# Inverting the odd layer's triangles by blocks of 16 instead of 32

## Chip, cores and metric

One core of one Trainium2 chip runs the whole program. The metric is device time in microseconds for one execution, lower is better. TensorE multiplies matrices, VectorE and ScalarE work on SBUF and on the products in PSUM, GpSimd (POOL) helps, and SyncE (SP) issues the transfers.

## What is computed

A decoder trunk of two layers on 1024 tokens of width 1024, in float32: an even layer (dilated window attention beside a gated linear recurrence), then an odd layer (gated DeltaNet), then a norm. The change lies in the odd layer. Per head and per chunk of 64 tokens the reference solves a unit lower triangular system:

```
lower = jnp.where(strict, jnp.einsum('bhnid,bhnjd->bhnij', kb, kc) * decay, 0.0)
a_mat = lower + jnp.eye(C_CHUNK, dtype=jnp.float32)
rhs = jnp.concatenate([vc * bc, kb * jnp.exp(gcum)[..., None]], axis=-1)
sol = lax.linalg.triangular_solve(a_mat, rhs, left_side=True, lower=True, unit_diagonal=True)
...
v_new = u_n - jnp.einsum('bhcd,bhdv->bhcv', w_n, state)
o = jnp.einsum('bhcd,bhdv->bhcv', qd_n, state) + jnp.einsum('bhij,bhjv->bhiv', a_n, v_new)
new_state = state * gl_n[..., None, None] + jnp.einsum('bhcd,bhcv->bhdv', kt_n, v_new)
```

The chunk length is free, as the result is the same recurrence; the kernel takes chunks of 128 tokens.

## The kernel before

The odd layer has 16 value heads that share 8 key heads. The kernel works on them in 8 pairs, `hh` = 0 to 7. For each pair it projects and convolves k, v and q (`proj`, `conv`), inverts the pair's 16 triangles of 128x128 (8 chunks by 2 heads; `invert`), and then walks the 8 chunks in turn (`recur`), where `ks`, `r`, `vp`, `vt`, `kv` and `S` form a chain over the chunks: TensorE, VectorE, TensorE, VectorE, and so on. `way_out` normalizes and gates a finished pair (`oz`, `ot`) and stores it for the last projection.

`invert` builds the triangles `L` from `kk`, the products of the keys, in two batches. It copies the 32x32 diagonal blocks to `Lg` and turns them with VectorE (`Lp`), so that each of the 128 partitions holds one block's column, 16 blocks of one partition group in the free dimension. A forward substitution of 31 steps on VectorE (`tm`, then `Tp`, two operations per step) inverts all 64 blocks at once. `Tn` and `Un` are the inverse and its transpose. From there TensorE doubles the block size with small products: `qp` and `up` from 32 to 64, `q2` and `u2` (in the trace `q` and `u`) from 64 to 128. All these products share one PSUM bank, tag "c". `T0`, the start of `Tp`, is loaded from a table of constants through SP.

TensorE's order is no loop nest. `invert` and `recur` are generators; `blend` and `mix` let projection work (`fill`) run between their steps. A step yields a need, in us of other work that should cover its latency, and what it does itself:

```
            for need, did in side:
                yield did
                debt += need * scale
```

A scheduler then fixes one order per engine when the program is built, from its own estimate of when operands are ready. In each engine's queue that order is kept on the chip. Hence every operation of the chain waits for whatever the order has put ahead of it on its engine.

While pair `hh` goes through `recur`, `invert(hh + 1)` and `proj(hh + 1)` run between its steps. Pair 0 is inverted ahead of all recurrences.

Of the kernel before, what the change touches and what calls it, by code (L numbers as in the profile page):

```python
# [9 lines left out]
F32 = mybir.dt.float32  # L10
F32R = mybir.dt.float32r
BF16 = mybir.dt.bfloat16
I32 = mybir.dt.int32
AF = mybir.ActivationFunctionType
ALU = mybir.AluOpType
# [3 lines left out]
P = 128  # L19
# [16 lines left out]
C_LV = C_MA + 128  # L36
C_ID32 = C_LV + 5 * 16
C_T0 = C_ID32 + 32
C_ALL = C_T0 + 512


def const_table():
    c = np.zeros((P, C_ALL), np.float32)
    p = np.arange(P)
    c[:, C_ID:C_ID + 128] = np.eye(P)

    a, q = p // 32, p % 32 * 4 + p // 32

    def count(dist):
        cnt = np.zeros(dist.shape, np.int64)  # L50
        for window, dil in ((128, 1), (512, 4), (2048, 16)):
# [12 lines left out]
    for lv in range(5):  # L64
        s = 1 << lv
        blk = j // s
        i = np.arange(32)
        odd = i[(i // s) % 2 == 1]
        c[:, C_LV + 16 * lv:C_LV + 16 * lv + 16] = (blk[:, None] % 2 == 0) & (blk[:, None] + 1 == odd[None, :] // s)
    c[:, C_ID32:C_ID32 + 32] = j[:, None] == np.arange(32)[None, :]  # L70

    i, j = np.arange(32)[:, None], np.arange(16)[None, :]
    for par in range(2):
        c[(p // 16) % 2 == par, C_T0:C_T0 + 512] = (i == 2 * j + par).reshape(-1)
    return c


# [1 line left out]
def trunk_kernel(ctx: ExitStack, tc: tile.TileContext, x, ew, ewo, ow, owab, owo, nw, fnw, lbl, hnw,  # L79
# [660 lines left out]
    def odd_layer(es):  # L740
        sp = es.enter_context(tc.tile_pool(name="od", bufs=1))
        gt = {n: sp.tile([P, NT, 16], F32, name=f"g_{n}") for n in ("beta", "gc", "ngc", "eg", "nbeg", "etl", "egl")}
        MA = sp.tile([P, 128], F32, name="MA")
        nc.sync.dma_start(MA, cst[:, C_MA:C_MA + 128])
        cws = sp.tile([P, 32, 4], F32, name="cws")
        nc.sync.dma_start(cws, cw)
        ow_ = sp.tile([P, 1], F32, name="onws")
# [219 lines left out]
        def invert(hh):  # L967
            kT = KT[hh]

            L = sp.tile([P, 16, 128], F32, name=f"L{hh}", tag="L", bufs=2)  # L970
            Lg = sp.tile([P, 16, 32], F32, name=f"Lg{hh}", tag="Lg")

            def decay_l(c):
                gcB = decays(hh, c, "l")

                for e in range(2):
                    act.activation(gcB[:, e, :], gcB[:, e, :], AF.Relu, bias=gt["ngc"][:, c, 2 * hh + e:2 * hh + e + 1])
                act.activation(gcB, gcB, AF.Exp, scale=-1.0)
                return gcB

            ahead_l = [decay_l(0)]
            for h in range(2):
                kk = bank("c", [P, 4, 128], f"kk{hh}_{h}")
                for c in range(4 * h, 4 * h + 4):
                    k_ = kT[:, c * 128:(c + 1) * 128]
                    pe.matmul(kk[:, c - 4 * h, :], k_, k_, start=True, stop=True)
                for c in range(4 * h, 4 * h + 4):
                    gcB = ahead_l.pop()
                    if c < NT - 1:
                        ahead_l.append(decay_l(c + 1))  # L990
                    for e in range(2):
                        dve.scalar_tensor_tensor(L[:, 2 * c + e, :], kk[:, c - 4 * h, :], SC[hh][:, 0, c, e:e + 1],
                                                 gcB[:, e, :], op0=ALU.mult, op1=ALU.mult)
                yield (15 if h else 7.0), 0.9


            for b in range(4):
                r = slice(32 * b, 32 * b + 32)
                act.copy(Lg[r], L[r, :, r])
            Lp = sp.tile([P, 32, 32], F32, name=f"Lp{hh}", tag="LpQ")  # L1000
            dve.transpose(Lp, Lg.rearrange("p u j -> p j u")[:, :, None, :].to_broadcast([P, 32, 2, 16]))
            Tp = sp.tile([P, 32, 16], F32, name=f"Tp{hh}", tag="Tp")
            nc.sync.dma_start(Tp, cst[:, C_T0:C_T0 + 512].rearrange("p (i j) -> p i j", i=32))
            for k in range(31):
                n = k // 2 + 1
                tm = sp.tile([P, 31, 16], F32, name=f"tm{hh}_{k}", tag="tm")
                dve.tensor_tensor(tm[:, :31 - k, :n], Lp[:, k, k + 1:, None].to_broadcast([P, 31 - k, n]),
                                  Tp[:, k:k + 1, :n].to_broadcast([P, 31 - k, n]), op=ALU.mult)
                dve.tensor_tensor(Tp[:, k + 1:, :n], Tp[:, k + 1:, :n], tm[:, :31 - k, :n], op=ALU.subtract)
            Tn = sp.tile([P, 16, 32], F32, name=f"Tn{hh}", tag="tm")  # L1010
            dve.transpose(Tn.rearrange("p u (j h) -> p j h u", h=2), Tp.rearrange("p i j -> p j i"))
            Un = sp.tile([P, 16, 32], F32, name=f"Un{hh}", tag="Lg")
            dve.transpose(Un, Tn)

            U = L
            T64 = sp.tile([64, 16, 64], F32, name=f"T64_{hh}", tag="T64")
            pool.memset(T64[0:32, :, 32:64], 0.0)
            for b in range(2, 4):
                r = slice(32 * b, 32 * b + 32)
                dve.tensor_copy(U[r, :, r], Un[r])  # L1020
            for b in range(2):
                r = slice(32 * b, 32 * b + 32)
                pool.tensor_copy(T64[r, :, r], Tn[r])

            a0, b0 = [slice(0, 32), slice(64, 96)], [slice(32, 64), slice(96, 128)]
            Q_ = sp.tile([P, 16, 64], F32, name=f"Q{hh}", tag="LpQ")
            qp = bank("c", [P, 16, 32], f"qp{hh}")
            for u in range(16):
                for r in range(2):
                    pe.matmul(qp[a0[r], u, :], L[b0[r], u, a0[r]], Un[b0[r], u, :], start=True, stop=True)  # L1030
            act.copy(Q_[a0[0], :, 0:32], qp[a0[0]])
            dve.tensor_copy(Q_[a0[1], :, 0:32], qp[a0[1]])
            yield 1.5, 1.3
            up = bank("c", [P, 16, 32], f"up{hh}")
            for u in range(16):
                for r in range(2):
                    pe.matmul(up[a0[r], u, :], Tn[a0[r], u, :], Q_[a0[r], u, 0:32], start=True, stop=True)
                pe.matmul(up[b0[0], u, :], Q_[a0[0], u, 0:32], Tn[a0[0], u, :], start=True, stop=True)
            act.mul(U[a0[1], :, b0[1]], up[a0[1]], -1.0)
            dve.tensor_scalar(T64[b0[0], :, 0:32], up[b0[0]], -1.0, None, op0=ALU.mult)  # L1040
            act.mul(U[a0[0], :, b0[0]], up[a0[0]], -1.0)
            for r in (1, 0):
                pool.memset(U[b0[r], :, a0[r]], 0.0)
            for b in range(2):
                r = slice(32 * b, 32 * b + 32)
                pool.tensor_copy(U[r, :, r], Un[r])

            yield 2.0, 1.8
            for h in range(2):

                q2 = bank("c", [P, 4, 64], f"q2{hh}_{h}")
                for u in range(8 * h, 8 * h + 8):
                    pe.matmul(q2[u % 2 * 64:u % 2 * 64 + 64, u // 2 % 4, :], L[64:128, u, 0:64], U[64:128, u, 64:128],
                              start=True, stop=True)
                for e in range(2):
                    (act.copy if h ^ e else dve.tensor_copy)(Q_[0:64, 8 * h + e:8 * h + 8:2, :], q2[64 * e:64 * e + 64])
                yield 1.2, 1.7
            for h in range(2):
                u2 = bank("c", [P, 4, 64], f"u2{hh}_{h}")
                for u in range(8 * h, 8 * h + 8):  # L1060
                    pe.matmul(u2[u % 2 * 64:u % 2 * 64 + 64, u // 2 % 4, :], T64[:, u, :], Q_[0:64, u, :], start=True, stop=True)
                for e in range(2):
                    d = U[0:64, 8 * h + e:8 * h + 8:2, 64:128]
                    if h ^ e:
                        act.mul(d, u2[64 * e:64 * e + 64], -1.0)
                    else:
# [203 lines left out]
```

## Time and profile before

| | |
|---|---|
| median of 3 runs | 2288.92 us (2286.33 to 2290.3) |
| profiled execution | 2290.27 us, its span 2288.5 us |
| TensorE busy, granted clock | 2171.9 us (95%), 0.993 |
| VectorE busy | 1427.0 us (62%) |
| substitution on VectorE (L1007, L1009) | 74.3 and 70.2 us in 2 x 248 operations |
| odd layer's inversions and recurrences | from about 1240 to 2126 us |

In the profile PE is TensorE, DVE VectorE, ACT ScalarE. A matmul of float32 operands shows as two records. A timeline row gives start, duration, engine, line, operation, tiles and shape, and in brackets the idle time before it and what ended it; a row of groups gives busy time, mean duration in ns of one, and idle time before; a row of windows gives a stretch, its length, and busy time of each engine with the number of records, the granted TensorE clock, the share of busy DMA and GB/s.

### The profile page before, as it was taken

What the parts mean: (1) busy time and instruction counts of PE and PEld (TensorE: products, weight loads), DVE (VectorE), ACT (ScalarE), POOL (GpSimd) and SP (SyncE); (2) the same over time, 40 slices, a digit from 0 to 9 for tenths busy, and PEclk for the clock granted to TensorE, in tenths of its full rate; (3) what the DMA queues carried; (4) which work ended last, traced back from release to release, by engine and by line L of the source; (5) the groups of instructions that cost most, each with busy time, mean ns of one, the idle gap of its engine ahead of it and who ended that gap; (6) DMA issues with size and microseconds to landing.
All of it is one profiled execution on the core that took longest, in us unless ns stands there. A gap on an engine that the chain in (4) does not pass through costs nothing. (4 is left out here: it accounts for less than half of the span.)

```text
span 2288.5 us, 54642 instructions
## 1 busy us (share of the span) xinstructions
PE 2171.9 (95%) x22597; PEld 1809.0 (79%) x22597; DVE 1427.0 (62%) x3364; ACT 963.4 (42%) x2623; POOL 226.5 (10%) x236
## 2 busy tenths in 40 slices
PE   7999999999999999988999988989899989899998
PEld 6888888898888888866887776767777767678787
DVE  6444444444444444456777887878788877855777
ACT  5333333333333332322236663755555555544223
POOL 0000000000000000000000012131212121210000
PEclk9999999999999999999999998999999999999999
DMA  4111111113222323352323221121212121214232
GB/s 145 38 48 48 44 47 48 43 39 95 78 82 84 90 83 92 97 160 88 102 97 104 59 56 62 53 79 46 76 43 76 52 74 59 65 60 148 91 113 109
DMA packets 101864, 175.83 MB, mean 77 GB/s; under 512 B 16752, under 2 KB 34032, under 8 KB 101616
## 3 DMA queue, kind: packets, MB, share of 16 engines
q1 hardware_dynamic: 101616, 172.35, 24.2%
q8 instruction: 177, 2.90, 0.5%
q14 instruction: 71, 0.58, 0.1%
HBM read 127.07 MB, written 25.23 MB: 67 GB/s over the span
## 5 line engine op out<-in xcount | busy, mean ns | idle before, releaser
L113 DVE TENSOR_TENSOR w_lo<-raww,w_hi 128x512 fp32r<-128x512 f32 x292 | 211.9, 727 | 151.1 <-ACT w_hi L112 147.1
L112 ACT CAST w_hi<-raww 128x512 fp32r<-128x512 f32 x292 | 181.1, 620 | 270.1 <-PE op L145 68.0
L143 PE MATMUL av<-w_hi,hn_hi 128*128 128x256 f32 x512 | 149.0, 291 | 0.0
L143 PE MATMUL bi<-w_hi,hn_hi 128*128 128x256 f32 x512 | 147.0, 287 | 0.0
L144 PE MATMUL bi<-w_lo,hn_hi 128*128 128x256 f32 x512 | 145.3, 284 | 0.0
L144 PE MATMUL av<-w_lo,hn_hi 128*128 128x256 f32 x512 | 144.8, 283 | 0.0
L145 PE MATMUL bi<-w_hi,hn_lo 128*128 128x256 f32 x512 | 144.8, 283 | 0.0
L145 PE MATMUL av<-w_hi,hn_lo 128*128 128x256 f32 x512 | 144.7, 283 | 0.0
L575 ACT ACTIVATE P<-P,nm 128x256 f32<-128x256 f32 (+7 forms) x128 | 71.4, 559 | 130.2 <-DVE nm L573 130.0
L143 PE MATMUL op<-w_hi,yplo 128*128 128x512 f32 x288 | 113.5, 394 | 1.6 <-DVE hr L273 0.9
L145 PE MATMUL op<-w_hi,yplo 128*128 128x512 f32 x288 | 112.2, 390 | 0.0
L144 PE MATMUL op<-w_lo,yplo 128*128 128x512 f32 x288 | 112.1, 389 | 0.0
L143 PE MATMUL pv<-hn_hi,w_hi 128*128 128x512 f32 x256 | 107.0, 418 | 2.6 <-ACT uv L822 2.6
L143 PE MATMUL oz<-hn_hi,w_hi 128*128 128x512 f32 x256 | 109.4, 427 | 0.0
L273 DVE TENSOR_TENSOR hr<-hr,op 128x512 f32<-128x512 f32 x128 | 86.1, 684 | 34.5 <-PE op L145 34.0
L145 PE MATMUL pv<-hn_hi,w_lo 128*128 128x512 f32 x256 | 104.3, 407 | 0.0
L144 PE MATMUL pv<-hn_lo,w_hi 128*128 128x512 f32 x256 | 102.6, 401 | 0.0
L144 PE MATMUL oz<-hn_lo,w_hi 128*128 128x512 f32 x256 | 102.3, 400 | 0.0
L145 PE MATMUL oz<-hn_hi,w_lo 128*128 128x512 f32 x256 | 102.0, 398 | 0.0
L581 DVE STREAM_TRANSPOSE PB<-P 128x256 f32<-128x256 f32 (+3 forms) x64 | 54.6, 854 | 74.9 <-ACT P L575 74.8
L143 PEld LDWEIGHTS av<-w_hi,hn_hi 128*128 128x128 f32 x512 | 97.9, 191 | 3.5 <-issue 1.9
L144 PEld LDWEIGHTS bi<-w_lo,hn_hi 128*128 128x128 f32 x512 | 98.1, 192 | 0.0
(354 smaller groups left out, 6044.9 us busy)
## 6 DMA issues: line engine op xcount, KB each, us to landing
raww<-in_ew_dram SPq DMA_DIRECT2D x128, 256.0 KB, 3.1
raww<-in_ow_dram SPq DMA_DIRECT2D x100, 256.0 KB, 3.0
V<-v SPq DMA_DIRECT2D x256, 64.0 KB, 2.0
rawy<-ymix SPq DMA_DIRECT2D x64, 256.0 KB, 2.7
raww<-in_ewo_dram SPq DMA_DIRECT2D x32, 256.0 KB, 3.0
gcl<-gcd SPq DMA_DIRECT2D x64, 128.0 KB, 3.0
gca<-gcd SPq DMA_DIRECT2D x64, 128.0 KB, 3.0
ymix<-oy SPq DMA_DIRECT2D x32, 256.0 KB, 2.0
```

What stands on the lines that cost most here:

```text
L112: act.copy(hi, raw)
L113: dve.tensor_tensor(lo, raw, hi.bitcast(F32), op=ALU.subtract)
L143: pe.matmul(ps, lh, rh, start=start, stop=False)
L144: pe.matmul(ps, lh, rl, start=False, stop=False)
L145: pe.matmul(ps, ll, rh, start=False, stop=stop)
L273: dve.tensor_tensor(dst[:, n], src[:, n], ps, op=ALU.add)
L575: act.activation(Pm[:, e, w0:], Pm[:, e, w0:], AF.Exp, bias=nmx[:, e:e + 1], scale=0.125, accum_out=den[:, i, e:e + 1])
L581: dve.transpose(PB[:, :, i * WG + w0:(i + 1) * WG], Pm[:, :, w0:])
```

## The change

The substitution stops at blocks of 16. The two 16x16 diagonal blocks of each 32x32 block are turned so that each partition holds a column of its own half: the transpose `Lp` is half as large, and a predicated copy with a mask `MH` (one column per half) moves the second half's rows into place. 15 steps instead of 31 follow, on at most 64 elements per partition instead of 136. ScalarE spreads the result over both halves with two masked copies, and `Tn` and `Un` are turned as before. Then comes the new doubling from 16 to 32: 64 products of 32x32 by 32x16 on the four diagonal places of the array (`sp0`), a masked copy on ScalarE (`Q0`, tile `Qs`), 64 more products (`sp1`), a subtraction into `Un`, and a second transpose that gives `Tn`. `Un` moves from `Lg`'s buffer to `Tp`'s. The need after the second batch of `kk` falls from 15 to 10, and the two new steps yield a need of 1.5 each. The load of `T0` halves; `MH` is a new small load at the layer's start.

```
-                yield (15 if h else 7.0), 0.9
+                yield (10 if h else 7.0), 0.9
...
-            Lp = sp.tile([P, 32, 32], F32, name=f"Lp{hh}", tag="LpQ")
-            dve.transpose(Lp, Lg.rearrange("p u j -> p j u")[:, :, None, :].to_broadcast([P, 32, 2, 16]))
+            Lp = sp.tile([P, 16, 32], F32, name=f"Lp{hh}", tag="LpQ")
+            dve.transpose(Lp, Lg.rearrange("p u (s j) -> p j s u", s=2))
+            dve.copy_predicated(Lp[:, :, 0:16], MH[:, 1:2, None].bitcast(I32).to_broadcast([P, 16, 16]), Lp[:, :, 16:32])
...
-            for k in range(31):
-                n = k // 2 + 1
-                tm = sp.tile([P, 31, 16], F32, name=f"tm{hh}_{k}", tag="tm")
-                dve.tensor_tensor(tm[:, :31 - k, :n], Lp[:, k, k + 1:, None].to_broadcast([P, 31 - k, n]),
-                                  Tp[:, k:k + 1, :n].to_broadcast([P, 31 - k, n]), op=ALU.mult)
-                dve.tensor_tensor(Tp[:, k + 1:, :n], Tp[:, k + 1:, :n], tm[:, :31 - k, :n], op=ALU.subtract)
+            for k in range(15):
+                n = k + 1
+                tm = sp.tile([P, 15, 16], F32, name=f"tm{hh}_{k}", tag="tm")
+                dve.tensor_tensor(tm[:, :15 - k, :n], Lp[:, k, k + 1:16, None].to_broadcast([P, 15 - k, n]),
+                                  Tp[:, k:k + 1, :n].to_broadcast([P, 15 - k, n]), op=ALU.mult)
+                dve.tensor_tensor(Tp[:, k + 1:16, :n], Tp[:, k + 1:16, :n], tm[:, :15 - k, :n], op=ALU.subtract)
+
+            act.mul(Tp[:, 16:32], Tp[:, 0:16], MH[:, 1:2])
+            act.mul(Tp[:, 0:16], Tp[:, 0:16], MH[:, 0:1])
             Tn = sp.tile([P, 16, 32], F32, name=f"Tn{hh}", tag="tm")
-            dve.transpose(Tn.rearrange("p u (j h) -> p j h u", h=2), Tp.rearrange("p i j -> p j i"))
-            Un = sp.tile([P, 16, 32], F32, name=f"Un{hh}", tag="Lg")
+            dve.transpose(Tn.rearrange("p u (s j) -> p j s u", s=2), Tp.rearrange("p i j -> p j i"))
+            Un = sp.tile([P, 16, 32], F32, name=f"Un{hh}", tag="Tp")
             dve.transpose(Un, Tn)
+
+            blk = [slice(32 * b, 32 * b + 32) for b in range(4)]
+            Q0 = sp.tile([P, 16, 16], F32, name=f"Qs{hh}", tag="LpQ")
+            sp0 = bank("c", [P, 16, 16], f"s0{hh}")
+            for u in range(16):
+                for r in blk:
+                    pe.matmul(sp0[r, u, :], Lg[r, u, :], Un[r, u, 16:32], start=True, stop=True)
+            act.mul(Q0, sp0, MH[:, 0:1])
+            yield 1.5, 1.4
+            sp1 = bank("c", [P, 16, 16], f"s1{hh}")
+            for u in range(16):
+                for r in blk:
+                    pe.matmul(sp1[r, u, :], Tn[r, u, :], Q0[r, u, :], start=True, stop=True)
+            dve.tensor_tensor(Un[:, :, 16:32], Un[:, :, 16:32], sp1, op=ALU.subtract)
+            dve.transpose(Tn, Un)
+            yield 1.5, 1.4
```

The scheduler makes a new order from this. On TensorE, around the first product that needs the inverted blocks of pair 5, this stood before (`pv` and `pk` are projections):

```order
L143 MATMUL pv_0_0_21964<-hn_hi_15183,w_hi_21213 128x512
L144 MATMUL pv_0_0_21964<-hn_lo_15185,w_hi_21213 128x512
L1030 MATMUL qp_21575<-Un_21566,L_21144 32x32 x32
L145 MATMUL pv_0_0_21964<-hn_hi_15183,w_lo_21214 128x512
...
L145 MATMUL pv_0_0_21964<-hn_hi_15183,w_lo_21214 128x512
L1105 MATMUL ks_5_21977<-S_4_21942,kT_19458 128x256
L1037 MATMUL up_21623<-Q_21574,Tn_21564 32x32 x2
```

and this stands there now, `s` being `sp0` (L1027) and `sp1` (L1033):

```order
L145 MATMUL pk_0_22353<-hn_lo_15185,w_hi_21648 128x512
L1027 MATMUL s_21908<-Un_21905,Lg_21592 32x16 x64
L1163 MATMUL op_3_22310<-vn_3_22292,A_3_22224 128x128 x2
L1114 MATMUL qk_4_22318<-q_21546,kT_19823 128x128
L1033 MATMUL s_22014<-Qs_21907,Tn_21903 32x16 x64
L1128 MATMUL ks_4_22371<-S_3_22307,kT_19823 128x256
L1134 MATMUL qs_4_22376<-S_3_22307,q_21546 128x256
L1053 MATMUL qp_22105<-Un_21905,L_21591 32x32 x32
L146 MATMUL pk_0_22353<-hn_hi_15183,w_lo_21649 128x512
```

The first product on the blocks has come a chunk earlier in the recurrence (3 instead of 4), one or two recurrence products stand behind each new pass, and `pk` is still being projected where `pv` was.

On VectorE, the end of the substitution of pair 5 stood so before:

```order
L1007 TENSOR_TENSOR tm_30_21561<-Lp_21467,Tp_21469 128x16
L1123 TENSOR_TENSOR vt_4_21917<-vp_4_21914,g_etl 128x256
L1009 TENSOR_TENSOR Tp_21469<-Tp_21469,tm_30_21561 128x16
L1011 STREAM_TRANSPOSE Tn_21564<-Tp_21469 128x32x16
L831 SCALAR_TENSOR_TENSOR kT_21894<-uk_21754,kT_21894 128x512
L1013 STREAM_TRANSPOSE Un_21566<-Tn_21564 128x512
...
L1020 COPY L_21144<-Un_21566 32x16x32 x2
L827 SCALAR_TENSOR_TENSOR kT_21894<-uk_21754,cws,kT_21894 128x512
...
L1032 COPY Q_21574<-qp_21575 32x16x32
```

and so now, with the `g` that ScalarE's masking has to let pass:

```order
L1011 TENSOR_TENSOR tm_14_21898<-Lp_21851,Tp_21854 128x15
L1013 TENSOR_TENSOR Tp_21854<-Tp_21854,tm_14_21898 128x15
L918 SCALAR_TENSOR_TENSOR g_1_1_22264<-g_1_1_22264,oz_1_1_22091 128x512
L1018 STREAM_TRANSPOSE Tn_21903<-Tp_21854 128x16x2x16
L1146 TENSOR_TENSOR vt_3_22290<-vp_3_22287,g_etl 128x256
L1020 STREAM_TRANSPOSE Un_21905<-Tn_21903 128x512
...
L1034 TENSOR_TENSOR Un_21905<-Un_21905,s_22014 128x16x16
L1131 SCALAR_TENSOR_TENSOR r_4_22373<-ks_4_22371,sc_19969,bv_21430 128x128
L1035 STREAM_TRANSPOSE Tn_21903<-Un_21905 128x512
L1043 COPY L_21591<-Un_21905 32x16x32 x2
...
L1055 COPY Q_22104<-qp_22105 32x16x32
```

The convolutions of `kT` that stood between `Un` and the copy of `Q` have moved behind it; the subtraction and a transpose have come in.

More of the change, by code (lines that the diff above doesn't have):

```diff
@@ L38 @@
 C_T0 = C_ID32 + 32
-C_ALL = C_T0 + 512
+C_MH = C_T0 + 256
+C_ALL = C_MH + 2
 def const_table():
@@ L70, in const_table @@
     c[:, C_ID32:C_ID32 + 32] = j[:, None] == np.arange(32)[None, :]
-    i, j = np.arange(32)[:, None], np.arange(16)[None, :]
-    for par in range(2):
-        c[(p // 16) % 2 == par, C_T0:C_T0 + 512] = (i == 2 * j + par).reshape(-1)
+    c[:, C_T0:C_T0 + 256] = np.eye(16).reshape(-1)
+    for half in range(2):
+        c[(p // 16) % 2 == half, C_MH + half] = 1.0
     return c
@@ L744, in odd_layer @@
         nc.sync.dma_start(MA, cst[:, C_MA:C_MA + 128])
+        MH = sp.tile([P, 2], F32, name="MH")
+        nc.sync.dma_start(MH, cst[:, C_MH:C_MH + 2])
         cws = sp.tile([P, 32, 4], F32, name="cws")
@@ L999, in invert @@
                 act.copy(Lg[r], L[r, :, r])
-            Lp = sp.tile([P, 32, 32], F32, name=f"Lp{hh}", tag="LpQ")
-            dve.transpose(Lp, Lg.rearrange("p u j -> p j u")[:, :, None, :].to_broadcast([P, 32, 2, 16]))
+            Lp = sp.tile([P, 16, 32], F32, name=f"Lp{hh}", tag="LpQ")
+            dve.transpose(Lp, Lg.rearrange("p u (s j) -> p j s u", s=2))
+            dve.copy_predicated(Lp[:, :, 0:16], MH[:, 1:2, None].bitcast(I32).to_broadcast([P, 16, 16]), Lp[:, :, 16:32])
             Tp = sp.tile([P, 32, 16], F32, name=f"Tp{hh}", tag="Tp")
-            nc.sync.dma_start(Tp, cst[:, C_T0:C_T0 + 512].rearrange("p (i j) -> p i j", i=32))
@@ L1004, in invert @@
-            for k in range(31):
-                n = k // 2 + 1
-                tm = sp.tile([P, 31, 16], F32, name=f"tm{hh}_{k}", tag="tm")
-                dve.tensor_tensor(tm[:, :31 - k, :n], Lp[:, k, k + 1:, None].to_broadcast([P, 31 - k, n]),
-                                  Tp[:, k:k + 1, :n].to_broadcast([P, 31 - k, n]), op=ALU.mult)
-                dve.tensor_tensor(Tp[:, k + 1:, :n], Tp[:, k + 1:, :n], tm[:, :31 - k, :n], op=ALU.subtract)
+            nc.sync.dma_start(Tp[:, 0:16], cst[:, C_T0:C_T0 + 256].rearrange("p (i j) -> p i j", i=16))
```

## The prediction

> **What bounds the kernel now.** I read the page first (busy times), then the windows view for one head pair cut into stages, then the windows of all eight inversions, then the timeline where a stage stood out.
>
> ```profile
> span 2288.5 us, 54642 instructions
> ...
> PE 2171.9 (95%) x22597; PEld 1809.0 (79%) x22597; DVE 1427.0 (62%) x3364; ACT 963.4 (42%) x2623; POOL 226.5 (10%) x236
> ```
>
> TensorE is 95% busy, so over the whole span it is the bound and VectorE's 62% looks harmless. The stages say otherwise. Here is the inversion of head pair 5: from the second batch of `kk` (1728.36) to the transpose `Lp`; from `Lp` to the end of `Un`, where the substitution runs; from `qp` to the last `u`; and the rest up to the next `kk`.
>
> ```profile
> core 0: us, PE busy (x) PEld busy (x) DVE busy (x) ACT busy (x) POOL busy (x), PEclk, DMA share, GB/s
> 1728.36:1742.20 13.84, 13.38 (x69) 11.14 (x70) 6.72 (x18) 11.29 (x31) 3.19 (x3) 1.00 0.41 133
> 1742.20:1776.20 34.00, 29.87 (x152) 23.51 (x150) 31.84 (x97) 18.08 (x63) 5.76 (x7) 1.00 0.17 53
> 1776.20:1791.50 15.30, 14.07 (x253) 10.69 (x252) 12.42 (x27) 9.48 (x35) 3.65 (x6) 1.00 0.14 44
> 1791.50:1824.80 33.30, 33.30 (x181) 28.15 (x181) 25.37 (x66) 16.58 (x43) 1.99 (x3) 1.00 0.14 40
> ```
>
> In the second row VectorE is busy 31.84 of 34.00 us and TensorE waits 4.1; in the fourth, where no substitution runs, TensorE is busy without a break. So the substitution is what makes VectorE the bound, for 34 us per pair. The same stage of all eight pairs:
>
> ```profile
> 1281.00:1323.10 42.10, 39.60 (x186) 32.16 (x184) 41.10 (x117) 23.67 (x69) 1.90 (x3) 1.00 0.15 47
> 1366.30:1405.40 39.10, 30.98 (x150) 23.73 (x150) 36.03 (x113) 19.08 (x61) 9.72 (x12) 0.92 0.14 44
> 1446.90:1494.60 47.70, 46.17 (x233) 36.86 (x231) 46.19 (x147) 30.33 (x94) 5.92 (x7) 1.00 0.13 40
> 1537.50:1573.70 36.20, 32.88 (x169) 26.49 (x167) 34.56 (x111) 21.72 (x83) 4.68 (x6) 1.00 0.15 45
> ...
> sum 301.30, PE 269.04 PEld 213.48 DVE 285.28 ACT 165.21 POOL 45.18; mean PE 33.63 PEld 26.69 DVE 35.66 ACT 20.65 POOL 5.65
> ```
>
> 301.30 - 269.04 = 32.3 us of idle TensorE is all that a lighter substitution can win in its own stage. Pair 1 (second row) holds 8.1 of it, and its clock column is 0.92. Its timeline, and the clock behind it:
>
> ```profile
> 1394.50 0.39 PE L144 MATMUL oz<-hn_lo,w_hi 128*128 128x512 f32 x1
> 1394.73 0.39 PE L145 MATMUL oz<-hn_hi,w_lo 128*128 128x512 f32 x1
> 1398.20 0.44 PE L935 MATMUL ot<-ident,bv 128*128 128x128 f32 x2 [3.08 <-POOL bv L928]
> ...
> 1405.43 1.92 PE L1030 MATMUL qp<-Un,L 32*32 32x32 f32 x64 [1.65 <-DVE Un L1013]
> ...
> 1407.87 0.63 PE L144 MATMUL oz<-hn_lo,w_hi 128*128 128x512 f32 x1
> 1408.30 0.63 PE L145 MATMUL oz<-hn_hi,w_lo 128*128 128x512 f32 x1
> ...
> 1399.70:1413.30 13.60, 11.29 (x183) 8.58 (x183) 8.47 (x15) 4.42 (x8) 9.06 (x11) 0.51 0.23 78
> ```
>
> TensorE ran dry at 1395, its clock was halved from 1399.7 to 1413.3, and 512-wide matmuls then followed each other at 0.43 us instead of 0.23.
>
> **The change, part by part.** *Substitution.* Prices of its rows:
>
> ```profile
> L1007 DVE TENSOR_TENSOR tm<-Lp,Tp 128x126 f32<-128x126 f32 (+22 forms) x31 | 9.4, 303 | 0.7
> L1009 DVE TENSOR_TENSOR Tp<-Tp,tm 128x126 f32<-128x126 f32 (+22 forms) x31 | 8.8, 285 | 0.6
> ...
> L1001 DVE STREAM_TRANSPOSE Lp<-Lg 128x1024 f32<-128x1024 f32 x1 | 2.0, 2018 | 1.8 <-ACT Lg L999 1.8
> ...
> 1758.10 0.28 DVE L1007 TENSOR_TENSOR tm<-Lp,Tp 128x136 f32<-128x136 f32 x1
> ...
> 1773.34 0.17 DVE L1007 TENSOR_TENSOR tm<-Lp,Tp 128x16 f32<-128x16 f32 x1
> ...
> 1773.96 1.12 DVE L1011 STREAM_TRANSPOSE Tn<-Tp 128x512 f32<-128x512 f32 x1
> ...
> 1775.54 0.68 DVE L1013 STREAM_TRANSPOSE Un<-Tn 128x512 f32<-128x512 f32 x1
> ```
>
> 0.17 us at 16 elements and 0.28 at 136 give 0.155 us + 0.00096 per element. Before: 62 operations on 2 x 2856 elements, 15.1 us undisturbed, 18.2 as measured (9.4 + 8.8); with the three transposes 22.0. After: 30 operations on 2 x 680 elements, 4.65 + 1.31 = 6.0. `Lp` halves to 128x512: between 0.68 and 1.12, taken 1.1 because its reading is strided as `Tn`'s. The predicated copy of 256 elements has no row: between 0.17 (a short operation) and 0.42 (`vt`, 128x256), taken 0.42 as the nearer. With `Tn` and `Un`, 9.3 us.
>
> *What stands between.* The larger of the other groups in that stage:
>
> ```profile
> L1133 DVE SCALAR_TENSOR_TENSOR S<-S,g_egl,kv 128x128 f32<-128x128 f32 x7 | 2.3, 336 | 0.0
> L827 DVE SCALAR_TENSOR_TENSOR kT<-uk,cws,kT 128x512 f32<-128x512 f32 x3 | 2.2, 749 | 0.0
> L113 DVE TENSOR_TENSOR w_lo<-raww,w_hi 128x512 fp32r<-128x512 f32 x3 | 2.0, 683 | 0.0
> L1108 DVE SCALAR_TENSOR_TENSOR r<-ks,sc,bv 128x128 f32<-128x128 f32 x6 | 2.0, 342 | 0.0
> L915 DVE SCALAR_TENSOR_TENSOR g<-g,oz 128x512 f32<-128x512 f32 x2 | 1.4, 680 | 0.0
> L1123 DVE TENSOR_TENSOR vt<-vp,g_etl 128x256 f32<-128x256 f32 x3 | 1.3, 420 | 0.1
> L1093 DVE TENSOR_TENSOR A<-qk,gca 128x256 f32<-128x256 f32 x3 | 1.3, 419 | 0.7 <-PE qk L1091 0.7
> ```
>
> In the order, 31 such operations lie between `Lp` and `Un` of pair 5 before (these, `bv` at `A`'s price, one more of `kT` and a short `cq`), at these means 14.3 us. With the undisturbed 15.1 + 3.8 that is 33.2, and the stage took 34.0, of which 0.7 is a wait for `qk`, so this pricing holds. Of the changed order 17 others remain: 4 `S`, 4 `r`, 2 each of `A`, `bv`, `vt`, `g`, and one `w_lo`, 7.3 us. Then ScalarE's two masking operations of 256 elements, taken 0.4 each as VectorE's of that size, hold `Tn` back, with ScalarE's own step for a 512-wide `g` between them in its order, taken 0.6 as the 512-wide copy of `Q` further down. VectorE's `g` covers some 0.5 of this 1.4: 0.9 us. The stage: 9.3 + 7.3 + 0.9 = 17.5 us.
>
> *What TensorE loses and gets.* The need after the second `kk` falls from 15 to 10, so 14.3 us of its work leaves the stage (45 matmuls of 0.23, and one chunk's `ks`, `qs`, `kv` with two chunks' `op`, `qk`, `vp` and 8 transposes) and runs later at the full pace of the fourth row. A pair changes by 17.5 + 14.3 - 34.0 = -2.2 us. Bounds: 29.87 - 14.3 = 15.6 us if TensorE paces the stage (-4.1), and 20.6 if its 51 operations cost the mean of today's 96 (34.0 / 96 = 0.354), with the 0.9 and the longest wait that `qp` shows, 1.65 in pair 1 (+0.9). Pairs 4 to 7: -8.8. Pair 3, with 16.6 moved: 17.5 + 16.6 - 36.2 = -2.1. Pair 2, 29.1 moved, others 7.8: -0.6. Pair 0, others 15.1, and 0.89 of the priced sum as in its own row (42.1 for 47.3): -0.7. Pair 1 keeps 19.7 us of others and moves 3.5: 9.3 + 19.7 + 0.9 + 3.5 - 39.1 = -5.7. Its dry spell I take as gone: the way from chunk 7's `op` to the first `ot` leads over eleven short VectorE operations between which substitution steps stand now and none will, and in the changed order 17 `oz` matmuls (3.9 us) with the `q` and `u` products fill it, where 14 `oz` alone did. So the half clock's cost behind 1405.4 goes too: nine matmuls by 0.20 and 1.1 us in `qp` and `up`, -2.9. Sum: -20.8.
>
> *The new products.* 64 instructions per pass are 128 records here (`qp`'s 32 are 64).
>
> ```profile
> L1030 PE MATMUL qp<-Un,L 32*32 32x32 f32 x512 | 10.3, 197 | 3.4 <-DVE Un L1013 2.3 <-DVE rt L191 0.5 <-DVE rt L190 0.5
> L408 PE MATMUL dg<-bq,bkt 128*32 128x32 f32 x512 | 6.1, 199 | 0.0
> ```
>
> `qp` uses two places of the array in turn: 10.3 / 512 = 20 ns a record. `dg` uses four, as the new passes do: 11.9 ns, and 9 without the last record's 0.19 us in each of its eight groups. At 9 ns a pass is 1.15 us, at `qp`'s 20 ns 2.6. I take 1.2 with the changeover, since the places are four and the rows are 16 wide instead of 32: 16 x 1.2 = +19.2. The Trainium skill (TensorE: Matmul & The Clock Gate, "Wait — 56ns, not 53.3ns?") says that start to start never drops below about 25 ns however small the matmul. By that rule a pass would be 3.2 us and the change a loss; the trace shows less than half of 25 ns in `dg`.
>
> *Waits in the new chain.* `sp0`, ScalarE's `Q0`, `sp1`, VectorE's subtraction, `qp`. The rows next to it:
>
> ```profile
> 1883.35 0.69 DVE L1013 STREAM_TRANSPOSE Un<-Tn 128x512 f32<-128x512 f32 x1
> 1884.10 1.20 PE L1030 MATMUL qp<-Un,L 32*32 32x32 f32 x64
> 1885.37 0.58 ACT L1031 COPY Q<-qp 32x512 f32<-32x512 f32 x1 [1.51 <-PE qp L1030]
> ...
> PE q L1053 <- ACT L L1041: 4.9, 6, 2.1
> PE up L1037 <- DVE Q L1032: 4.6, 5, 1.5
> ```
>
> A handover costs 0.06 to 0.07 us, `Q0` 0.4, the subtraction 0.42; the order puts 0.67 us of `op` and `qk` behind `sp0` and 0.86 of `ks` and `qs` behind `sp1`, which covers both if ScalarE and VectorE are free. Queued behind the waiting `qp` is all of TensorE. I take 0.1 each, +1.6 in all; bounds 0 and 0.6 (what `up` waits in pair 5). Of the 9.5 us that `up` and `q` wait now, I take 4 as gone: their copies stand behind `kT` convolutions, and in the changed order those come after `Q`. -4.0, between 0 and -9.5. The second transpose of `Tn` (0.7) lies beside `qp`.
>
> *Loads.* `Tp`'s load halves, but `Un` now sits in `Tp`'s buffer, so on SP the next pair's load waits for `qp` and for POOL's copies out of `Un`, some 8 us later, with weight loads and `gca` behind it (an estimate from the two passes, the subtraction and `qp`). I cost it at nothing: weights are fetched a unit ahead. If that cover failed, `raww` would be late. The mask load is one issue.
>
> Sum: -20.8 - 4.0 + 19.2 + 1.6 = -4.0 us on the profiled execution's 2290.27 (its span 2288.5 and 1.8 around it): 2286. It lay 1.35 above the median of the three runs (2288.92), so against that median 2285, and I say 2284 as the bounds reach further down than up.
>
> **The rivals.**
> *VectorE's pace vanishes* (faster): the stage falls to TensorE's 15.6. For it: 9.3 + 7.3 = 16.6 is close to it. Pairs 4 to 7 then give -16.4, 3 -3.3, 2 -1.5, 0 -2.5, 1 -8.1 and -2.9; passes at 1.05 us 16.8; with -4.0 and +1.6: -20, 2269.
> *TensorE reaches `sp0` before `Un`* (slower): its cover is 14.3 us shorter, and it waits there with all its work queued behind. For it: the substitution was measured at 18.2 us and not at its undisturbed 15.1, and a wait can halve the clock as in pair 1. If the stage takes 20.6 in pairs 2 to 7: 6 x 3.1 = +18.6, and a half clock of a few us now and then, 2304. It decides from 18.2 us on, where six pairs give back the 4.0. Against it: `qp` came within 0.06 us of `Un` (1883.35 + 0.69 to 1884.10) with VectorE pacing both.
> *The passes do not overlap* (slower): at `qp`'s 20 ns, 16 x 1.4 more, 2306; by the skill's 25 ns, 16 x 2.0 more, 2316. Against it: `dg`.
> *Pair 1's hole stays* (same): POOL's `bv` behind VectorE's `ors` is still what `ot` waits for. +8.6, 2293.
>
> **How the numbers follow.** Forecast 0.40, its own range 2278 to 2290, half of it beyond 0.2% (4.6 us, about what a measurement of this kernel tells from no change); pace vanishes 0.20; `sp0` waits 0.20; no overlap 0.05; hole stays 0.15, mostly within 0.2%. Faster 0.20 + 0.21 = 0.41, same 0.18 + 0.13 = 0.31, slower 0.28. The range runs from the second case to the third: 2268 to 2304.
>
> **What would show it.** The stage from `Lp` to `Un` at 16 to 18.5 us in pairs 3 to 7; 30 substitution operations of 0.2 us; each new pass at 1.1 to 1.4 us; no `ot` wait of 3 us and no half clock near 1400; waits at `sp1` and `qp` under 0.3. I am wrong if waits for `Un` at `sp0` pass 1 us per pair, if a pass passes 2 us, or if VectorE was not what held TensorE in the second row.

## The result and the profile after

The changed kernel took 2320.66 us (median of 4 runs, 2318.05 to 2322.84), beside 2289.61 for the kernel before (4 runs): a ratio of 1.0131, with a 95% interval of 1.0117 to 1.0145. It is slower by 31 us. The forecast was 2284, in a range from 2268 to 2304, so the prediction was wrong, in sign too.

The head of the page after. TensorE's busy time grew by 47.8 us, VectorE's fell by 56.1:

```profile
span 2321.1 us, 58572 instructions
...
PE 2219.7 (96%) x24645; PEld 1853.9 (80%) x24645; DVE 1370.9 (59%) x3132; ACT 971.0 (42%) x2647; POOL 221.5 (10%) x236
```

The windows view for the inversion of pair 5, cut as before, but with the stretch from the end of `Un` to the last `u` in two rows: up to the first `up`, and from there on.

```profile
core 0: us, PE busy (x) PEld busy (x) DVE busy (x) ACT busy (x) POOL busy (x), PEclk, DMA share, GB/s
1748.33:1762.50 14.17, 13.01 (x66) 10.52 (x66) 6.65 (x18) 10.78 (x30) 2.94 (x3) 1.00 0.39 131
1762.50:1779.40 16.90, 15.23 (x78) 12.13 (x78) 15.25 (x52) 10.87 (x33) 4.07 (x4) 1.00 0.16 51
1779.40:1791.53 12.13, 9.98 (x340) 7.71 (x338) 5.56 (x13) 2.97 (x10) 4.37 (x7) 0.79 0.26 69
1791.53:1804.90 13.37, 13.17 (x184) 10.63 (x184) 5.29 (x10) 6.51 (x25) 0.00 (x0) 0.81 0.01 1
1804.90:1850.86 45.96, 45.96 (x243) 38.80 (x244) 37.62 (x87) 24.33 (x73) 7.92 (x8) 1.00 0.15 44
```

The second row, from `Lp` to `Un`, fell from 34.00 to 16.90 us; the last grew from 33.30 to 45.96, as the moved projection work runs there. Up to here the pair gains 17.1 - 12.7 = 4.4 us. The third and the fourth row together are 25.50 us where 15.30 stood, and their clock columns, 1.00 before, are 0.79 and 0.81. That is where the time went: 10.2 us more in this pair. The timeline of that place:

```profile
1779.72 1.26 PE L1027 MATMUL s<-Un,Lg 32*32 32x16 f32 x128
1780.91 0.71 PE L1163 MATMUL op<-vn,A 128*128 128x128 f32 x4
1781.46 0.39 PE L1114 MATMUL qk<-q,kT 128*128 128x128 f32 x2
1781.78 0.66 PE L1033 MATMUL s<-Qs,Tn 32*32 32x16 f32 x56
1784.32 0.78 PE L1033 MATMUL s<-Qs,Tn 32*32 32x16 f32 x72 [1.88 <-issue]
1785.03 0.70 PE L1128 MATMUL ks<-S,kT 128*128 128x256 f32 x2
...
1788.84 0.63 PE L144 MATMUL pk<-hn_hi,w_hi 128*128 128x512 f32 x1
1789.26 0.63 PE L145 MATMUL pk<-hn_lo,w_hi 128*128 128x512 f32 x1
```

The first pass takes 1.19 us to the next instruction, as priced. The second stops after 56 of its 128 records for 1.88 us, and the releaser is "issue": nothing that the profile shows was waited for. From 1786 on the projection's matmuls follow each other at 0.42 us instead of 0.23: half clock. The waits view of TensorE from 1230 us on shows the same stop in every pair:

```profile
PE s L1033 <- issue: 12.7, 8, 2.5
PE qp L1053 <- issue: 0.3, 1, 0.3
```

The page's section on DMA queues names what was missing. Before, and then after:

```profile
q8 instruction: 177, 2.90, 0.5%
```

```profile
q8 instruction: 193, 3.16, 0.6%
```

Queue 8 brings TensorE's code: 2 x 22597 matmuls and weight loads in 177 packets before are 255 instructions a packet, 2 x 24645 in 193 after also 255, and 16 more packets are one for each new pass. A pass is 128 matmul records and 128 weight loads, one packet's worth, used up in 1.2 us. By the trace's record of that queue a packet was issued at 1781.17 and had landed at 1783.16; TensorE went on at 1784.32. Counting TensorE's instructions from the start (matmuls, weight loads and the waits between them), all nine stops of this kernel come at a number that is 193 above a multiple of 256, to within one. (The Trainium skill, Runtime: NRT & Kernel Launch, "Instruction fetch mechanics", says that code comes in blocks of 256 instructions, the next while the current one runs, and that this is mostly hidden. The trace agrees on the blocks; for these passes they are not hidden.)

The half clock, in stretches of 3.41 us, in which it comes and goes in this trace:

```profile
1779.49:1782.90 3.41, 2.95 (x192) 2.47 (x191) 1.77 (x5) 1.17 (x5) 0.00 (x0) 1.00 0.60 153
1782.90:1786.32 3.42, 2.00 (x90) 1.59 (x91) 0.98 (x3) 0.12 (x1) 0.62 (x2) 1.00 0.16 49
1786.32:1789.73 3.41, 3.14 (x66) 2.69 (x60) 2.72 (x5) 1.68 (x5) 3.21 (x5) 0.51 0.10 21
1789.73:1793.14 3.41, 3.41 (x95) 2.57 (x96) 0.00 (x0) 0.00 (x0) 0.54 (x2) 0.50 0.07 22
1793.14:1796.56 3.42, 3.42 (x28) 2.87 (x23) 1.11 (x2) 1.35 (x3) 0.00 (x0) 0.50 0.03 5
1796.56:1799.97 3.41, 3.21 (x43) 2.41 (x43) 0.42 (x1) 1.60 (x7) 0.00 (x0) 0.99 0.00 0
```

The first row holds the first pass, and the clock stays full behind it; the second holds the stop, and the clock halves behind it. It is so in seven of the eight pairs: the stretch ahead of the half clock has the stop or part of it in it, with 0.8 to 2.5 us of idle TensorE. (In pair 2 it has a wait of 1.8 us for `Un` ahead of the first pass.) In pair 6 even a stretch in which TensorE runs 239 records without idle time keeps its clock, and the next one does not:

```profile
1892.18:1895.59 3.41, 3.41 (x239) 2.91 (x240) 2.04 (x6) 0.99 (x5) 0.00 (x0) 1.00 0.54 142
1895.59:1899.01 3.42, 1.26 (x51) 1.06 (x40) 0.45 (x2) 0.18 (x2) 0.14 (x1) 1.00 0.18 57
```

So in this kernel half clock follows the idle time beside the small products, the stops' above all.

The granted clock is either full or half in these traces. Over the whole span its mean was 0.993 before and is 0.978 now: 2 x 0.007 x 2288.5 = 32 us at half clock then, 2 x 0.022 x 2321.1 = 102 us now. Seventy microseconds more at half clock can cost up to 35.

### The profile page after: what moved, and what is told of

Same layout as the page of the kernel before. It is cut to its first block, busy times and chain, and to the rows that moved or that the text cites. A ratio compares the mean times of both kernels' runs of the same rounds, so it can differ in the third digit from the quotient of the medians.

```text
span 2321.1 us, 58572 instructions
## 1 busy us (share of the span) xinstructions
PE 2219.7 (96%) x24645; PEld 1853.9 (80%) x24645; DVE 1370.9 (59%) x3132; ACT 971.0 (42%) x2647; POOL 221.5 (10%) x236
## 4 chain that ended last, share of the span: by engine, by line
PE 72%; DVE 11%; DMA 8%; ACT 6%; issue 3%; POOL 0%; SPq 0%; DVEq 0%; ACTq 0%; POOLq 0%
PE op L144 4%; PE op L146 4%; PE op L145 4%; DMA gcl<-gcd 3%; PE av L144 3%; PE av L145 3%; PE av L146 3%; PE bi L146 2%; PE bi L145 2%; PE bi L144 2%; PE o L596 2%; PE pv L144 2%; PE pv L145 2%; PE pv L146 2%; DMA raww<-in_ew_dram 2%
## 5 line engine op out<-in xcount | busy, mean ns | idle before, releaser
L1102 POOL TENSOR_TENSOR gca<-gca,MA 128x256 f32<-128x256 f32 x64 | 50.8, 793 | 513.9 <-DMA gca<-gcd 390.7
```

What stands on the lines that cost most here:

```text
L1102: pool.tensor_tensor(DA, DA, MA[:, None, :].to_broadcast([P, 2, 128]), op=ALU.add)
```

## The experiments

The theory from here on is called "bursts": the two passes are too many small instructions in one go, first for the code supply (holes), then for the clock. The rival "cover" says that the moved projection work no longer covers the chain of handovers. All twelve runs, below the two kernels, with the same two measures (half clock is 2 x (1 - clock) x span); the medians of before beside them were 2290.8 to 2293.8:

| run | us | ratio to before, 95% | clock | half clock, us | waits for issue at `s` and `qp`, us |
|---|---|---|---|---|---|
| before | 2289.6 | | 0.993 | 32 | 0 |
| changed | 2320.7 | 1.0131 (1.0117 to 1.0145) | 0.978 | 102 | 13.0 |
| e1_wide | 2270.9 | 0.9906 (0.9891 to 0.9921) | 0.993 | 32 | 0 |
| e2_halves20 | 2330.3 | 1.0166 (1.0150 to 1.0181) | 0.986 | 65 | 0 |
| e3_need20 | 2323.4 | 1.0133 (1.0109 to 1.0158) | 0.983 | 79 | 10.8 |
| e4_one_place | 2377.9 | 1.0380 (1.0362 to 1.0399) | 0.967 | 156 | 0 |
| e5_half | 2275.0 | 0.9916 (0.9890 to 0.9941) | 0.994 | 27 | 2.0 |
| e6_before_plus | 2347.6 | 1.0232 (1.0204 to 1.0260) | 0.975 | 117 | 15.6 |
| e7_wide20 | 2274.4 | 0.9913 (0.9889 to 0.9936) | 0.994 | 27 | 0 |
| e8_junk | 2375.5 | 1.0349 (1.0299 to 1.0399) | 0.967 | 157 | 0 |
| e9_spaced | 2285.9 | 0.9979 (0.9967 to 0.9991) | 0.987 | 60 | 2.2 |
| e10_bf16 | 2281.2 | 0.9954 (0.9939 to 0.9970) | 0.991 | 41 | 0 |
| e11_junk4 | 2374.7 | 1.0364 (1.0336 to 1.0392) | 0.995 | 24 | 0 |
| e12_spaced_bf16 | 2280.0 | 0.9948 (0.9929 to 0.9966) | 0.992 | 36 | 0 |

### The passes or the rest: e1_wide and e6_before_plus

```diff
-            for u in range(16):
-                for r in blk:
-                    pe.matmul(sp0[r, u, :], Lg[r, u, :], Un[r, u, 16:32], start=True, stop=True)
+            pe.matmul(sp0.rearrange("p u j -> p (u j)"), Lg[:, 0:4, :].rearrange("p u j -> p (u j)"), Un[:, :, 16:32], ...)
...   (sp1 likewise)
```

> Each of the two new passes is one matmul of 128x256 instead of 64 small ones; the doubling from 16 to 32 is left out, everything around it stays. Theory (bursts): the changed kernel lost its time where the small products come in a burst, because TensorE's instructions arrive in pieces of 16 KB and the burst outruns them (12.7 us of waits put down to issue at the second pass), and because the clock is halved behind it (103 us of half clock against 34 before). Then both go: waits for issue under 2 us, half clock under 45 us, and with 16 x 0.75 us of product time saved the time is 2255 to 2272. Rival (cover): the time went because 14 us of other work per pair no longer cover the chain of handovers; then only the product time goes, about 2309.

2270.9 us, as the theory had it; "cover" would have been 2309. Its timeline at the place of the passes:

```profile
1750.88 0.59 PE L1025 MATMUL s<-Un,Lg 128*128 128x256 f32 x2
1751.31 0.61 PE L1159 MATMUL op<-vn,A 128*128 128x128 f32 x4
```

A wide matmul stands for 0.43 us, 7 in all. So the sixteen passes cost 1.31% + 0.94% of 2290 = 51.5 us, and 7: 58 us, where the forecast had 20.8. And everything else in the change together gave 21.5 + 7 = 28 us, where the forecast had 24.8.

From the other side, two unread passes put into the kernel before:

```diff
             dve.transpose(Un, Tn)
+            for u in range(16):
+                for r in blk:
+                    pe.matmul(sp0[r, u, :], Tn[r, u, :], Un[r, u, 16:32], start=True, stop=True)
+            yield 1.5, 1.4
...   (a second pass the same way)
```

> The kernel before with the full substitution in blocks of 32, and two passes of 64 small products per pair put between Un and qp, whose results nobody reads; no operation on ScalarE or VectorE between them. Theory (bursts): the passes alone carry the loss whatever the substitution does: 16 x 1.2 us of products, 8 to 16 us of waits for issue and some 70 us more of half clock, together 45 to 65 us: 2335 to 2355. Rival (the price of the products alone, as forecast): 19 us more, 2305 to 2312.

2347.6, 2.32% or 53 us over before, with the old substitution untouched. Its waits view:

```profile
PE s L1024 <- issue: 13.7, 8, 2.2
```

All ten of its stops, and all eight of e3_need20, come at an instruction number 193 above a multiple of 256 too, again to within one. The passes carry the loss.

### More cover: e3_need20 and e7_wide20

```diff
-                yield (10 if h else 7.0), 0.9
+                yield (20 if h else 7.0), 0.9
```

> The need after the second kk is 20 instead of 10 and nothing else. Theory (bursts): the two passes still follow each other with three matmuls between them, so waits for issue stay at 8 to 16 us, half clock at 80 us or more, and the time at 2312 to 2328. Rival (cover): the chain is covered again, and the time falls to 2285 to 2300.

> The run with one wide matmul per pass (the doubling left out), with the need after the second kk at 20 instead of 10. It tells why need 20 did not help: theory, the larger need has a price of its own, since it takes projection work from the recurrence's handovers: 2278 to 2292 against 2270.9 with need 10. Rival, it has none: 2266 to 2275, and then what need 20 left over in the two runs with products is not explained by it.

2323.4 with the passes, 2274.4 without. Twice the need does not help the one and costs the other nothing that can be measured (0.9913 beside 0.9906): the theory's side thought that need 20 had a price of its own, and that was wrong. "Cover" is not what was lost.

### Slower passes without a hole: e4_one_place

```diff
-            for u in range(16):
-                for r in blk:
+            for r in blk:
+                for u in range(16):
```

> The loops over the places and over the triangles are exchanged in the two new passes: sixteen products in turn on the same place of the array instead of four places in turn. The same instructions, taken more slowly: an estimate of 40 ns a record, twice what qp shows on two places, is 5.1 us a pass, 62 us more in all. Two readings of the half clock: if the hole of 2 us that the missing instructions leave is what halves it, the holes shrink to under 4 us in all, the half clock falls to 50 us or less, and the time is 2320 to 2350; if the little work that small products give the array is what halves it, half clock is 100 us or more and the time is 2360 to 2420.

2377.9, and no wait for issue at all, yet 156 us of half clock. Pair 5's passes, and then two stretches of 3.4 us, one inside the first pass and the next one:

```profile
1813.57 4.40 PE L1027 MATMUL s<-Un,Lg 32*32 32x16 f32 x128
1817.90 1.22 PE L1163 MATMUL op<-vn,A 128*128 128x128 f32 x4
1818.92 0.64 PE L1114 MATMUL qk<-q,kT 128*128 128x128 f32 x2
1819.48 6.45 PE L1033 MATMUL s<-Qs,Tn 32*32 32x16 f32 x128
```

```profile
1813.30:1816.70 3.40, 3.40 (x110) 3.13 (x109) 1.07 (x3) 0.00 (x0) 0.00 (x0) 0.99 0.58 153
1816.70:1820.10 3.40, 3.40 (x43) 3.14 (x41) 0.85 (x2) 0.95 (x4) 0.00 (x0) 0.50 0.02 6
```

TensorE is busy for all of 3.40 us and the clock halves behind it. So a half clock does not need a hole: small products that give the array little to do are enough, where they fill a stretch at this slow pace. It does not follow that the changed kernel would lose its clock without the stops, since there the first passes, at 1.19 us, kept it. (The Trainium skill, TensorE: Matmul & The Clock Gate, "HAM oscillation — how this bites in real kernels", has as the abstract rule that TensorE should have no idle gap over some 3.4 us. Here the clock halves without a gap, and the measurement decides.)

### What the clock counts: e8_junk and e11_junk4

```diff
                     pe.matmul(sp0[r, u, :], Lg[r, u, :], Un[r, u, 16:32], start=True, stop=True)
+                if u % 2 == 1:
+                    pe.matmul(jk0, hn("hi", 0, slice(0, 128)), hn("hi", 1, slice(0, 256)), start=True, stop=True)
```

> After every second triangle of the two new passes stands one matmul of 128x128 by 256 columns whose result nobody reads, eight per pass; the order of everything else is as in the changed kernel, and all products are there. It slows a pass as the run on one place did, but with work for the whole array. If little use of the array is what halves the clock: half clock 55 us or less, waits for issue under 3 us, and the time 2300 to 2325 with some 20 to 35 us of added work in it. If it is the number of small instructions, or something that follows them: half clock stays at 90 us or more and the time is 2335 to 2360.

2375.5 with 157 us of half clock: a miss. By its words the count of small instructions had it, though the time is above that range too. But the count alone does not decide: a stretch inside a pass holds about 100 of them here and in e4_one_place and loses its clock, while the changed kernel's stretch of 239 records above, nearly all of them small, kept it. The timeline of e8_junk shows why the work added was little: sixteen records and one wide matmul take 0.55 us, where sixteen records of a plain pass take 0.15 (an estimate from 9.3 ns each) and 256 columns of a projection 0.11 (half of 0.23).

```profile
1817.38 0.31 PE L1028 MATMUL s<-Un,Lg 32*32 32x16 f32 x16
1817.62 0.38 PE L1030 MATMUL s<-hn_hi 128*128 128x256 f32 x1
1817.93 0.31 PE L1028 MATMUL s<-Un,Lg 32*32 32x16 f32 x16
```

So I weighed each record by its columns and by the share of the 128 rows it fills (twice for the f32 ones, whose two records each take about twice as long per column as the projection's), and summed over each stretch of 3.41 us. That predicted how e11_junk4, with four wide matmuls in place of one, would differ:

> As the run with one unread matmul of 128x256 after every second triangle, but with four of them. Reading (use of the array): weighing every matmul by its columns and by the share of the 128 rows that it fills, a stretch of 3.41 us at full clock turned to half clock in nearly all cases where the sum lay under some 2900, and the one unread matmul gave about 2350 per stretch; four give some 4400. So half clock falls from 159 us to under 55, though a pass then takes some 7 us, 93 us more than in the changed kernel in all, and the time is 2355 to 2385. Rival (the mixture of small and large products, or their count, halves the clock): half clock over 140 us and the time over 2415.

```profile
1813.86 0.31 PE L1028 MATMUL s<-Un,Lg 32*32 32x16 f32 x16
1814.10 0.74 PE L1031 MATMUL s<-hn_hi 128*128 128x256 f32 x4
1814.77 0.31 PE L1028 MATMUL s<-Un,Lg 32*32 32x16 f32 x16
```

24 us of half clock instead of 157, and 2374.7 us instead of 2375.5: 384 more wide matmuls cost nothing that can be measured, since they bought back the clock. Over all fourteen traces, from 1100 us on, 103 of 4747 stretches at full clock were followed by half clock. A bound of 2896 on this sum, counted as below, puts 17 of the 4747 on the wrong side; the best bound on idle time puts 45 there, and the best on the number of 32x32 records 102, which is hardly better than none. (A stretch of projection matmuls alone sums to 7680.) From 50 us on, with the even layer, it is 29 and 55 of 9002. The bound is fitted to these same traces, but leaving e11_junk4 out gives the same one. The exact count that the clock goes by is not shown.

### Half a burst: e5_half and e10_bf16

```diff
-            for u in range(16):
+            for u in range(0, 16, 2):
```

> Only every second of the 16 triangles of a place goes through the two new passes: 32 products in each instead of 64 (half of the doubling from 16 to 32 is left out, with its part of the ScalarE and VectorE operations). Theory (bursts): it is the length of the burst that counts, so half of it costs far less than half: no waits for issue, half clock 35 to 70 us, time 2276 to 2292. Rival (a fixed price per product): halfway between the run with one wide matmul per pass, 2270.9, and the changed kernel, 2320.7: 2296, with half clock near 70 us.

2275.0, just under its range, with 27 us of half clock, also under its own; but there are 2.0 us of waits for issue at `qp`, where none was expected. By the ratios, 32 products in each pass cost 2 + 7 us more than none (0.9916 beside 0.9906, and the wide matmuls' 7), the next 32 some 49 us (1.0131 beside 0.9916). So the price is no fixed one per product; where between 32 and 64 it rises is not shown.

```diff
+            LT = sp.tile([P, 2, 16, 32], mybir.dt.bfloat16, name=f"LT{hh}", tag="T64")
+            pool.tensor_copy(LT[:, 0], Lg)
...
+            QU = sp.tile([P, 2, 16, 16], mybir.dt.bfloat16, name=f"Qs{hh}", tag="LpQ")
+            Q0, Ur = QU[:, 0], QU[:, 1]
+            act.copy(Ur, Un[:, :, 16:32])
+            dve.tensor_copy(LT[:, 1], Tn)
```

> The 64 products of each pass take copies of their operands in bf16 (one copy more on POOL, one on ScalarE, one on VectorE per pair), so that TensorE gets 128 instructions per pass instead of 256 for the same 64 products; the result of the doubling is rounded accordingly. Theory (bursts): what counts is how many of TensorE's instructions come in one go; a pass takes about 0.6 us, no waits for issue, half clock 30 to 70 us: 2274 to 2292. Rival (the number of small products, however coded): holes and half clock as in the changed kernel, 2308 to 2325.

2281.2, with all 64 products. In bf16 a product is one record and one weight load instead of two of each, and a pass is shorter by half:

```profile
1759.70 0.64 PE L1032 MATMUL s<-Qs,LT 32*32 32x16 bf16 x64
1760.27 0.49 PE L1119 MATMUL qk<-q,kT 128*128 128x128 f32 x2
```

### Bursts cut or pulled apart: e2_halves20, e9_spaced, e12_spaced_bf16

In these three, edges in the order (not waits) hold the next matmuls of the projection behind a burst, and the next burst behind them. In the first each pass is cut in two:

```diff
-            for u in range(16):
-                for r in blk:
-                    pe.matmul(sp0[r, u, :], ...)
+            for u0 in range(0, 16, 8):
+                m = ORD.pop("m", None)
+                with tc.issue_after(m) if m is not None else ExitStack():
+                    for u in range(u0, u0 + 8):
+                        for r in blk:
+                            pe.matmul(sp0[r, u, :], ...)
+                if u0 + 8 < 16:
+                    ORD["a"] = last_pe()
+                    yield 1.7, 0.3
```

> Each new pass is cut in two halves of 32 products, two thirds of a microsecond or more of projection matmuls are forced between the halves, and the need after the second kk is 20 instead of 10 so that this work is there. Same arithmetic, same number of products. Theory (bursts): waits for issue under 3 us in all, half clock under 60 us, 2280 to 2298. Rival (cover): gains no more than the run with need 20 alone, whatever the halves do.

2330.3: a miss, and by its words the rival had it. The holes are gone and half clock is down to 65 us, yet it is slower than the changed kernel, and no faster than e3_need20 with the same need (1.0166 and 1.0133, intervals overlapping). Its waits view for the period of pair 5 shows what came instead:

```profile
PE kv L1173 <- DVE vt L1167: 2.5, 1, 2.5
PE up L1081 <- DVE Q L1076: 1.5, 1, 1.5
```

With 0.8 each for `ks` and `q` these are some 5.6 us in a pair. Not all of it comes from the halves: `kv` waits for `vt` 13.4 us in all here, but 15.6 in e3_need20 and 15.4 in e7_wide20, which have the same need, and 5.7 in the changed kernel. What e3_need20 does not have is 10.9 us at `up` for `Q`, and 9.6 us for `Un` once, in pair 0. That the forced projection work stands apart from the handovers that it used to cover would explain `up`; no run shows it alone.

In the second the passes stay whole, and some twelve projection matmuls stand behind each:

```diff
             act.mul(Q0, sp0, MH[:, 0:1])
-            yield 1.5, 1.4
+            if hh >= 2:
+                ORD["a"] = last_pe()
+            yield (3.2 if hh >= 2 else 1.5), 1.4
...   (the same behind sp1; the need of 10 is 28 from pair 2 on)
```

> Both passes whole and with all products, but pulled apart: from pair 2 on about 12 projection matmuls are forced between the first and the second pass and as many between the second and qp, and the need after the second kk is 28 there, so that this work is at hand. Theory (bursts): each burst of 64 products then has more than 3.4 us to itself, so waits for issue fall under 3 us and half clock under 55 us; the larger need was free in the run with wide matmuls (2274.4), to which 16 x 0.85 to 1.1 us of products come: 2284 to 2298. Rival: as in the run cut into halves the forced order leaves the recurrence's handovers bare and new waits (for vt, for Q) take the gain: 2310 to 2330.

2285.9, 0.9979 of before (0.9967 to 0.9991): faster than both kernels, with the same arithmetic as the changed one. Pair 5:

```profile
1773.99 1.26 PE L1036 MATMUL s<-Un,Lg 32*32 32x16 f32 x128
1775.17 0.71 PE L1158 MATMUL vp<-r,L 128*128 128x128 f32 x4
...
1779.67 1.26 PE L1045 MATMUL s<-Qs,Tn 32*32 32x16 f32 x128
1780.86 0.50 PE L144 MATMUL pv<-hn_hi,w_hi 128*128 128x512 f32 x1
```

Neither pass has a hole, the two lie 5.7 us apart, and no half clock follows here, though the stretch of the first pass holds 128 of its records:

```profile
1773.66:1777.07 3.41, 3.41 (x140) 2.84 (x139) 3.34 (x7) 2.56 (x7) 0.04 (x1) 1.00 0.02 5
```

The half clock of the whole run, 60 us, is above the 55 that were expected. But the waits for issue lie in pairs 0 and 1, which are not spaced, and from 1430 to 2100 us, which is pair 2 on, half clock is 17 us where the changed kernel has 61. From one pair's `kk` to the next, pair 5 takes 104.8 us, beside 112.8 in the changed kernel and 106.7 before.

> Both cures together: the passes pulled apart from pair 2 on with need 28, and the products in bf16. Theory: holes and half clock are gone already with either, so together they give little more than bf16 alone, the price of the pass halved against the spaced run: 2270 to 2284. If it lies above 2284, the forced order has a price that the spaced run hid.

2280.0, no clear difference from bf16 alone (0.9948 and 0.9954, intervals overlapping): as far as this tells, both cures take away the same thing.

## Why the prediction was wrong

The step that failed is **the new products**, "16 x 1.2 = +19.2", with 1.6 for waits. The 1.2 us is right for a pass by itself (1.19). But the term counted the time of the records and not their number nor their use of the array. It measured 58 us: 19 for the products, 13.0 for code that had not arrived, and the remaining 26 lie with 70 us more of half clock, which can cost up to 35. How the 39 divide exactly is not shown, since no run took away the one alone at an unchanged pace. Two of the prediction's own signs of being wrong show it: the second pass of pair 5 takes 3.25 us to the next instruction, where a pass over 2 was named, and the wait inside it is 1.88 us, where under 0.3 was expected at `sp1`.

Both could have been asked of the trace of before. Its queue 8 held 177 packets of 16 KB for 2 x 22597 instructions, so a pass of 256 records and weight loads uses up a packet in 1.2 us. And pair 1's half clock was read there as the price of a wait, while `qp` and `up` beside it, small products as well, also gave the array little to do. The Trainium skill's floor of 25 ns (TensorE: Matmul & The Clock Gate, "Wait — 56ns, not 53.3ns?"), weighed against the row of `dg`, was rightly set aside: a record takes 1.19 / 128 = 9.3 ns on four places.

The other steps, by what the traces show. The stage from `Lp` to `Un` in pairs 3 and 7, first and last of those forecast at 16 to 18.5 us:

```profile
1538.00:1554.90 16.90, 15.19 (x78) 12.13 (x78) 15.26 (x52) 10.86 (x33) 3.99 (x4) 1.00 0.17 52
...
1986.60:2003.30 16.70, 15.26 (x78) 12.14 (x78) 15.09 (x52) 8.72 (x27) 4.06 (x4) 1.00 0.15 48
```

Right, against 17.5. The substitution's rows in pair 5:

```profile
L1013 DVE TENSOR_TENSOR Tp<-Tp,tm 128x15 f32<-128x15 f32 (+7 forms) x15 | 4.0, 268 | 0.2
L1011 DVE TENSOR_TENSOR tm<-Lp,Tp 128x15 f32<-128x15 f32 (+7 forms) x15 | 3.4, 230 | 0.3
```

7.4 us for 30 operations, where 6.0 stood (0.25 us each instead of 0.2), and 18 others between instead of 17 (one `w_lo` more). The 6.0 was an undisturbed price; before, the rows came to 18.2 where that price was 15.1, much the same excess. The stage still came out at 16.9 because neighbouring records overlap: all its groups on VectorE sum to 18.6 us, and VectorE is busy for 15.25. VectorE and TensorE end the stage nearly level, 15.25 and 15.23 us busy, so the rival in which VectorE's pace vanishes was close. The moved work came back at 12.7 us in the last row instead of 14.3. TensorE's waits at `up` and `q` fell from 9.5 to 1.7 us, where 4 of them were taken as gone. Pair 1's period fell by 8.1 us (83.1 to 75.0 from `kk` to `kk`), where -5.7 and -2.9 were forecast and +2.6 for its two passes and their waits; its dry spell is gone, though 6.8 us of half clock follow the stretch with the stop in its second pass. Of the rivals, "The passes do not overlap" gave the times nearest to the result (2306 and 2316), but not its cause: the 1.19 us refute it. "TensorE reaches `sp0` before `Un`" gave 2304, and its wait came once, 1.8 us for `Un` at `sp0` in pair 2.

## What to carry to other kernels

Price a group of small matmuls by three numbers, not one: its time, its number of instructions against the packets of code in which they arrive (here 256 instructions, and a packet took 0.9 to 2.1 us to land and over 1 us more to act), and the array work left in the few microseconds around it. Put large matmuls between such groups, without taking them from a chain that they cover, or halve the instructions, where the rounding to bf16 can be borne; the 58 us of these passes then fell to some 24 (pulled apart) and 18 (in bf16). And when a kernel's clock column falls, look for what came before in the array's use, not only for idle time.

## What was not expected of the hardware

Code supply can stop TensorE in the middle of a run of independent matmuls: 27 stops in three kernels, all 193 instructions past a multiple of 256 (to within one), of 0.3 to 2.5 us, nine of them 13.0 us in the changed kernel, where TensorE went on 1.1 to 1.6 us after the packet had landed. The clock can halve behind a stretch of 3.41 us in which TensorE never idles (e4_one_place), and wide matmuls whose result nobody reads can pay for themselves (e11_junk4 against e8_junk).
